# Strassen's block products for two up-projection quarters, and weight block sums made by accumulating DMAs

## The chip, the cores and the metric

One of the eight cores of a Trainium2 chip runs the whole program. The metric is device time in microseconds (us) for one execution; of the kernel before there are three timed runs and one profiled execution. The engines are named as in the profile: PE (matmuls), PEld (its weight loads), DVE (vector), ACT (scalar), POOL (GpSimd) and SP, which here only issues DMAs.

## What is computed

A decoder trunk of two layers on 512 tokens of 1024 features. Each layer has a mixer (a convolution with a state-space scan in the first, gated linear attention in the second), cross-attention into 256 memory tokens, and an MLP, each followed by a LayerNorm of `ALPHA * x + f(x)`. The change is about the MLP, of which the reference says:

```
def sq_relu_mlp(x, w1, w2):
    return jnp.square(jax.nn.relu(x @ w1)) @ w2

h = layer_norm(DEEPNORM_ALPHA * h + sq_relu_mlp(h, mlp_w1[i], mlp_w2[i]), ln_g[i, 2], ln_b[i, 2])
```

`w1` is 1024 x 4096, `w2` is 4096 x 1024, all in float32.

## The kernel before

**Three matmuls for one.** Each operand is held as a pair in a rounded form that PE takes at full rate: `hi`, a cast copy made on ACT, and `lo`, the rest, made on DVE as source minus `hi` (`split`, L104 to L107). A product is then hi x hi, hi x lo and lo x hi (`mm3`, L156 to L160). Weights come from DRAM by 1 MB loads on SP's queue and pass through `wpair`: two pieces of 128x1024 for each megabyte, one ACT cast and one DVE subtraction each. The pools for these pieces (`wh`, `wl`) hold six each.

**The up projection** makes feature tiles: the weight pair is the stationary operand, the 512 tokens stream past. A quarter of the 4096 features is 8 tiles x 8 pieces of the inner dimension x 3 = 192 matmuls of 512 columns (`feat_tiles`). ACT then does Relu and Square on each tile and writes it into a tile `ab`. The first four tiles of a quarter 0 are made in two halves of 256 tokens (`halves=4`), because the second half of the tokens is still being transposed.

**The down projection** takes the first three quarters by one level of Strassen's algorithm in Winograd's form (`strassen`, L537 to L587). A quarter's 1024x1024 weights are cut into four blocks of 512x512, its 512 tokens into two halves, and seven block products of 24 matmuls with 512 columns do what eight would. The sums of weight blocks are DVE subtractions (`blk_sub`, L524 to L527, in two pieces of 128x1024 each, four sums in a quarter). The sums of activation blocks are DVE instructions too (L567 to L577), and so are the additions of the products into the residual tiles `h` and the shared product `E` (L547 to L559). The last quarter goes through `out_proj`, whose LayerNorm follows.

**What sets the order.** The instructions of each engine are laid down in one order when the program is built, by a list scheduler that knows the data dependences; at run time each engine takes its own in that order and waits on semaphores. Between the block products of a quarter lie the up tiles of the next (`mlp`: two tiles of quarter `qd + 1` ahead of `strassen`, six behind it), so that in the built order they can mix.

Of the kernel before, what the change touches and what calls it, by code (L numbers as in the profile page):

```python
# [22 lines left out]
ALPHA = (2 * DEPTH) ** 0.25  # L23
# [6 lines left out]
class Trunk:  # L30
# [253 lines left out]
    def bcast_row(self, row, tag):  # L284
        t = self.cp.tile([P, D], F32, tag=tag, name=self.nm(tag))
        self.nc.sync.dma_start(t, row.rearrange("(o d) -> o d", o=1).broadcast_to([P, D]))
        return t
# [7 lines left out]


    def begin_ln(self, i, j):
        g = self.bcast_row(self.aps["ln_g"][i, j], "lng")
        b = self.bcast_row(self.aps["ln_b"][i, j], "lnb")
# [118 lines left out]
    def xa(self, i, h, xT, kT, v):  # L418
# [78 lines left out]

    def blk_load(self, w, r, c, stays=True):  # L500
# [14 lines left out]
    def sa(self, shape):
        return self.mp.tile(shape, F32R, tag="sa", bufs=4, name=self.nm("sa"))

    def blk_a(self, src):
        t = self.sa([P, 2, 4, 256])
# [16 lines left out]
    def strassen(self, w, r0, A, h, E, first, last):  # L536
# [4 lines left out]
        X = self.blk_load(w, r0, 0)  # L541

        def add(t, hf, begin):
            def f(i, ps):
                y = h[t + i, hf]
                if begin and first:
                    v.scalar_tensor_tensor(y, y, ALPHA, ps, ALU.mult, ALU.add)  # L547
                else:
                    v.tensor_tensor(y, y, ps, ALU.add)
# [11 lines left out]
        pa = [self.ps.tile([P, S], F32, tag="acc", name=self.nm("acc")) for _ in range(2)]  # L561
        self.blk_prod(pa, self.blk_a(A1[:, :, t0]), self.blk_w(X), True, e1)
        self.blk_prod(pa, self.blk_a(A2[:, :, t0]), self.blk_w(self.blk_load(w, r0 + S, 0, False)), False, add(0, 0, True))
        B12 = self.blk_load(w, r0, S)
        self.blk_sub(X, B12, X)
        Sx = self.mp.tile([P, 4, 256], F32, tag="sx", bufs=2, name=self.nm("sx"))
        v.tensor_tensor(Sx, A1[:, :, t1], A2[:, :, t1], ALU.add)  # L567
        pc = [self.accb() for _ in range(2)]
        self.blk_prod(pc, self.blk_a(Sx), self.blk_w(X), True, add(2, 1, True))
        B22 = self.blk_load(w, r0 + S, S)  # L570
        self.blk_sub(X, B22, X)
        v.tensor_tensor(Sx, Sx, A1[:, :, t0], ALU.subtract)
        pb = [self.aux() for _ in range(2)]
        self.blk_prod(pb, self.blk_a(Sx), self.blk_w(X), True, e2)
        self.blk_sub(B12, B22, B12)
        v.tensor_tensor(Sx, A2[:, :, t0], Sx, ALU.subtract)
        v.tensor_tensor(A1[:, :, t1], A1[:, :, t0], A1[:, :, t1], ALU.subtract)  # L577
        self.blk_prod(pc, self.blk_a(Sx), self.blk_w(B22), False, add(0, 1, True))
        self.blk_sub(X, self.blk_load(w, r0 + S, 0, False), X)
        pd = [self.ps.tile([P, S], F32, tag="acc", name=self.nm("acc")) for _ in range(2)]  # L580
        self.blk_prod(pd, self.blk_a(A1[:, :, t1]), self.blk_w(B12), True, add(2, 1, False))
        self.blk_prod(pd, self.blk_a(A2[:, :, t1]), self.blk_w(X), False, add(2, 0, True))
        if last:
            for i in range(2):
                for y in (h[i, 1], h[2 + i, 1], h[2 + i, 0]):
                    v.tensor_tensor(y, y, E[i], ALU.add)

    def mlp(self, i, h, xT):
        nc = self.nc
        w1, w2 = self.aps["mlp_w1"][i], self.aps["mlp_w2"][i]  # L590
        NQ = 4
        A = {}

        r2 = []

        def pair(m):
            if m % 4 == 0:
                hl = [self.sa([P, 4, S]) for _ in range(2)]
                r2.extend([(hl[0][:, k, :], hl[1][:, k, :]) for k in range(4)])
            self.split(A[NQ - 1, m // 4][:, m % 4, :], *r2[m])  # L600

        def up(qd, m0, n, halves=0, pairs=False):
# [693 lines left out]
```

## Time and profile before

| | us |
|---|---|
| timed runs | 1610.10, 1605.85, 1609.43 (median 1609.43) |
| the profiled execution, its own time | 1611.48 |
| its span from first to last instruction | 1609.8 |
| PE busy | 1581.7 (98%) |
| DVE busy | 1067.8 (66%) |
| ACT busy | 703.7 (44%) |
| POOL busy | 338.6 (21%) |
| DMA queues, share of 16 engines' span | 35.2% (SP's queue) |

The profile is of one execution. Busy shares are over the whole span; a matmul's duration includes the time in which it overlaps its neighbours, so the pace of PE is read from the starts of successive matmuls. The MLP of layer 0 takes about 543 to 876 us of the span, that of layer 1 has the same form near the end.

### The profile page before, as it was taken

To read this page: it belongs to the slowest core of one execution; us is meant where nothing else is said; L and a number is where in the kernel's file an instruction comes from. 1 tells how busy PE (TensorE), PEld (TensorE's weight loads), DVE (VectorE), ACT (ScalarE), POOL (GpSimd) and SP (SyncE) were. 2 spreads that over 40 slices of the span, in tenths; PEclk is the share of its full clock that TensorE was granted. 3 is DMA by queue.
4 is the path that set the end of the run, shared out by engine and by line. 5 is a ranking of instruction groups with operands and counts; after the bars stand their busy time and mean duration, and the time that the engine had idled before them with its cause. 6 is when DMAs were issued, how large, how long until landed. Compare 5 with 4: busy or idle time off the path is not lost.

```text
span 1609.8 us, 19786 instructions
## 1 busy us (share of the span) xinstructions
PE 1581.7 (98%) x7866; PEld 1327.8 (82%) x7866; DVE 1067.8 (66%) x1372; ACT 703.7 (44%) x1087; POOL 338.6 (21%) x266
## 2 busy tenths in 40 slices
PE   8999999999999999999999999999999999999998
PEld 7878888788988988888888788898988988888886
DVE  3997999883755676676837544444754767676835
ACT  3346547661332454545442534352342354545440
POOL 5745837744101200000001121222201200000000
PEclk9999999999999999999999999999999999999999
DMA  7223336633521515152233331267321525242221
GB/s 250 97 80 107 104 105 190 200 108 105 209 79 52 185 53 183 53 166 70 79 105 98 118 105 60 98 217 248 98 93 32 191 66 166 70 157 79 79 79 53
DMA packets 136864, 188.50 MB, mean 117 GB/s; under 512 B 6966, under 2 KB 82918, under 8 KB 136771
## 3 DMA queue, kind: packets, MB, share of 16 engines
q1 hardware_dynamic: 136162, 187.03, 35.2%
q8 instruction: 62, 1.02, 0.3%
q0 software_dynamic: 608, 0.20, 0.1%
q14 instruction: 32, 0.25, 0.0%
HBM read 176.69 MB, written 10.52 MB: 116 GB/s over the span
## 4 chain that ended last, share of the span: by engine, by line
PE 90%; DVE 5%; DMA 2%; POOL 1%; issue 1%; ACT 1%; SPq 0%; DVEq 0%; POOLq 0%; ACTq 0%
PE acc L159 18%; PE acc L160 18%; PE acc L158 18%; PE accb L160 8%; PE accb L159 8%; PE accb L158 8%; DVE cv L948 2%; PE aux L160 2%; PE aux L158 2%; PE aux L159 2%; DVE h L319 1%; DMA ws<-in_even_w_in_dram 1%; PE aux L279 1%; PE aux L874 1%; DMA t<-acsd 0%
## 5 line engine op out<-in xcount | busy, mean ns | idle before, releaser
L106 ACT CAST wh<-ws 128x1024 fp32r<-128x1024 f32 x238 | 249.1, 1051 | 420.5 <-PE acc L160 122.5
L107 DVE TENSOR_TENSOR wl<-ws,wh 128x1024 fp32r<-128x1024 f32 x178 | 224.8, 1266 | 255.8 <-ACT wh L106 255.8
L159 PE MATMUL acc<-t,wh 128*128 128x512 f32 (+1 forms) x800 | 288.8, 362 | 3.9 <-POOL t L374 3.1
L158 PE MATMUL acc<-t,wh 128*128 128x512 f32 (+1 forms) x800 | 290.0, 364 | 0.3 <-ACT t L106 0.3
L160 PE MATMUL acc<-t,wl 128*128 128x512 f32 (+1 forms) x800 | 289.8, 363 | 0.0
L107 POOL TENSOR_TENSOR wl<-ws,wh 128x1024 fp32r<-128x1024 f32 x60 | 148.3, 2481 | 297.1 <-ACT wh L106 286.3
L159 PEld LDWEIGHTS acc<-t,wh 128*128 128x128 f32 x800 | 154.0, 193 | 26.1 <-POOL t L374 3.3
L158 PEld LDWEIGHTS acc<-t,wh 128*128 128x128 f32 x800 | 153.3, 192 | 23.2 <-issue 1.6
L160 PEld LDWEIGHTS acc<-t,wl 128*128 128x128 f32 x800 | 153.7, 192 | 22.2 <-issue 1.0
L158 PE MATMUL acc<-wh,t 128*128 128x512 f32 x424 | 168.3, 397 | 0.5 <-ACT t L106 0.5
L159 PE MATMUL acc<-wl,t 128*128 128x512 f32 x424 | 167.3, 395 | 0.0
L160 PE MATMUL acc<-wh,t 128*128 128x512 f32 x424 | 166.5, 397 | 0.3 <-DVE t L107 0.3
L948 DVE SCALAR_TENSOR_TENSOR cv<-u,cw,cv 128x491 f32<-128x491 f32 (+29 forms) x210 | 146.6, 729 | 1.0
L160 PE MATMUL accb<-t,wl 128*128 128x512 f32 (+1 forms) x368 | 126.9, 345 | 0.0
L158 PE MATMUL accb<-t,wh 128*128 128x512 f32 (+1 forms) x368 | 126.6, 345 | 0.0
L159 PE MATMUL accb<-t,wh 128*128 128x512 f32 (+1 forms) x368 | 126.6, 344 | 0.0
L106 ACT CAST wh<-sq 128x1024 fp32r<-128x1024 f32 x72 | 75.2, 1049 | 96.5 <-PE acc L160 34.0
L314 POOL TENSOR_TENSOR s<-s,mhalf 128x1 f32<-128x1 f32 x24 | 23.2, 967 | 429.9 <-DVE s L313 429.9
L107 DVE TENSOR_TENSOR wl<-sq,wh 128x1024 fp32r<-128x1024 f32 x72 | 87.6, 1221 | 35.2 <-ACT wh L106 35.2
L106 ACT CAST t<-aux 128x512 fp32r<-128x512 f32 (+1 forms) x84 | 44.8, 547 | 147.2 <-PE aux L279 121.7
L158 PE MATMUL acc<-wh,sa 128*128 128x512 f32 x272 | 107.5, 395 | 0.0
L160 PE MATMUL acc<-wh,sa 128*128 128x512 f32 x272 | 107.4, 395 | 0.0
(336 smaller groups left out, 3006.2 us busy)
## 6 DMA issues: line engine op xcount, KB each, us to landing
ws<-in_mlp_w_dram SPq DMA_DIRECT2D x52, 1024.0 KB, 5.3
sq<-in_mlp_w_dram SPq DMA_DIRECT2D x18, 1024.0 KB, 5.1
ws<-in_even_w_in_dram SPq DMA_DIRECT2D x17, 1024.0 KB, 5.1
ws<-in_odd_w_in_dram SPq DMA_DIRECT2D x12, 1024.0 KB, 5.1
ws<-in_xa_w_k_dram SPq DMA_DIRECT2D x8, 1024.0 KB, 4.9
ws<-in_xa_w_v_dram SPq DMA_DIRECT2D x8, 1024.0 KB, 5.5
kvd<-kv SPq DMA_DIRECT2D x32, 256.0 KB, 3.2
ws<-in_even_w_out_dram SPq DMA_DIRECT2D x8, 1024.0 KB, 5.0
```

The lines of the kernel that those rows point to most:

```text
L106: self.last_hi = nc.scalar.copy(hi, src)
L107: (eng or nc.vector).tensor_tensor(lo, src, hi.bitcast(F32), ALU.subtract)
L158: nc.tensor.matmul(out, a[0], b[0], start=start, stop=False, skip_group_check=more)
L159: nc.tensor.matmul(out, a[0], b[1], start=False, stop=False, skip_group_check=more)
L160: nc.tensor.matmul(out, a[1], b[0], start=False, stop=stop, skip_group_check=more)
L279: nc.tensor.transpose(ps[:, j * P:(j + 1) * P], halves[hf][:, j * P:(j + 1) * P], self.ident)
L314: nc.gpsimd.tensor_tensor(r, r, self.mhalf[:, :1], ALU.pow)
L319: nc.vector.scalar_tensor_tensor(y, y, r, ln["b"][:, sl], ALU.mult, ALU.add)
L874: last = nc.tensor.matmul(py[:, i * 64:(i + 1) * 64], Ms[i // 4][:, (i % 4) * P:(i % 4 + 1) * P], xdt[:, i * 64:(i + 1) * 64], start=True, ...
L948: nc.vector.scalar_tensor_tensor(cs[j][:, s:], u[m][:, :S - s], w[:, 30 - s:31 - s], cs[j][:, s:], ALU.mult, ALU.add)
```

## The change

Quarters 1 and 2 of the up projection become seven block products as well (`up_blocks`). Here the transposed activations are the moving operand, so a block product has 256 tokens as columns: 2 x 2 feature tiles x 4 pieces x 3 = 48 matmuls of 256 columns. The activation sums, which are the same for both quarters, are made once in a layer (`up_sums`). One function, `blk_unit`, runs the seven products for up and down in the order 1, 2, 5, 7, 6, 3, 4. The signs are arranged so that every weight sum is an addition, and `blk_sub` is gone: the tile X holds block 11 for product 1, then takes on block 12 (product 5), block 22 (product 6) and block 21 (product 4), each by a DMA with `accum_op=ALU.add` that POOL issues (`blk_add`). The tile T3 takes one such addition ahead of product 7. A unit so has four plain loads of 1 MB and four accumulating ones; there are three down units and two up units in a layer, 40 accumulating DMAs in all.

The rows of `ln_g` and `ln_b` for the MLP's LayerNorm move to a tile of the tag `sq`. The final quarter's up tiles now all follow the last down unit; no up tiles stand between block products any more.

The core of the diff:

```diff
-    def blk_sub(self, dst, a, b):
-        for j in range(2):
-            ks = slice(2 * j, 2 * j + 2)
-            self.nc.vector.tensor_tensor(dst[:, ks, :], a[:, ks, :], b[:, ks, :], ALU.subtract)
+    def blk_add(self, st, w, r, c):
+        self.nc.gpsimd.dma_start(st, w[r:r + S, c:c + S].rearrange("(k p) c -> p k c", p=P), accum_op=ALU.add)
...
+    def blk_unit(self, w, r, c, prod, op, out):
+        X = self.blk_load(w, r, c)
+        T3 = self.blk_load(w, r, c + S)
+        self.blk_add(T3, w, r + S, c + S)
+        pa = [self.ps.tile([P, S], F32, tag="acc", name=self.nm("acc")) for _ in range(2)]
+        prod(pa, op(1), self.blk_w(X), True, out[1])
+        self.blk_add(X, w, r, c + S)
+        prod(pa, op(2), self.blk_w(self.blk_load(w, r + S, c, False)), False, out[2])
+        pc = [self.accb() for _ in range(2)]
+        prod(pc, op(5), self.blk_w(X), True, out[5])
+        self.blk_add(X, w, r + S, c + S)
+        pd = [self.ps.tile([P, S], F32, tag="acc", name=self.nm("acc")) for _ in range(2)]
+        prod(pd, op(7), self.blk_w(T3), True, out[7])
+        pb = [self.aux() for _ in range(2)]
+        prod(pb, op(6), self.blk_w(X), True, out[6])
+        self.blk_add(X, w, r + S, c)
+        prod(pc, op(3), self.blk_w(self.blk_load(w, r + S, c + S, False)), False, out[3])
+        prod(pd, op(4), self.blk_w(X), False, out[4])
+    def blk_prod_t(self, pss, a, w, start, evac):
+        for i in range(2):
+            for j in range(2):
+                m = slice((2 * i + j) * P, (2 * i + j + 1) * P)
+                o = pss[i][:, j * 256:(j + 1) * 256]
+                for k in range(4):
+                    self.mm3(o, (w[k][0][:, m], w[k][1][:, m]), (a[0][:, k, :], a[1][:, k, :]),
+                             start and j == 0 and k == 0, k == 3, not start or j == 1)
+            evac(i, pss[i])
...
+        A = self.ab()
+        up(A, 0, 0, 4, halves=4)
+        ops = self.up_sums(tiles)
+        up(A, 0, 4, 4)
         for qd in range(NQ - 1):
-            last = qd == NQ - 2
-            up(qd + 1, 0, 2)
-            self.strassen(w2, qd * D, [A[qd, 0], A[qd, 1]], h, E, qd == 0, last)
-            if last:
-                pair(0)
-                pair(1)
-            up(qd + 1, 2, NK - 2, pairs=last)
+            if qd > 0:
+                A = self.ab()
+                self.up_blocks(w1, qd * D, ops, A)
+            self.down_blocks(w2, qd * D, A, h, E, qd == 0, qd == NQ - 2)
+        A = self.ab()
+        up(A, (NQ - 1) * D, 0, NK, pairs=True)
```

**The built order, on DVE.** First the kernel before, in the second block quarter of layer 0 (`sq` holds weight blocks, `wl` is a `lo` piece, in brackets the semaphores waited for; DMAHW are those of SP's DMAs, DMASW those of POOL's):

```order
L107 TENSOR_TENSOR wl_5821<-sq_5813,wh_5820 128x1024 [waits DMAHW3_49,PE_49,Activation_49]
L527 TENSOR_TENSOR sq_5813<-sq_5893,sq_5813 128x1024 [waits DMAHW4_49,DVE_49]
L527 TENSOR_TENSOR sq_5893<-sq_5938,sq_5893 128x1024 [waits DMAHW5_49,DVE_49]
L107 TENSOR_TENSOR wl_5825<-sq_5813,wh_5824 128x1024 [waits PE_49,Activation_49]
L527 TENSOR_TENSOR sq_5813<-sq_5893,sq_5813 128x1024 [waits DVE_49]
L527 TENSOR_TENSOR sq_5893<-sq_5938,sq_5893 128x1024 [waits DVE_49]
```

Then the changed kernel (its line numbers are some 90 higher), in the second down unit of layer 0, from product 5's weights to product 6's; `sq_5952` is X, `sq_5954` is T3:

```order
L107 TENSOR_TENSOR wl_6044<-sq_5952,wh_6043 128x1024 [waits DMASW4_49,Activation_49]
L107 TENSOR_TENSOR wl_6048<-sq_5952,wh_6047 128x1024 [waits Activation_49]
L650 TENSOR_TENSOR E_4830<-E_4830,acc_5957 128x512 [waits PE_49]
L663 TENSOR_TENSOR sx_6038<-ab_5506,ab_5507 128x1024 [waits Activation_49]
L107 TENSOR_TENSOR wl_6085<-sq_5954,wh_6084 128x1024 [waits DMASW2_49,DVE_49,Activation_49]
L650 TENSOR_TENSOR E_4831<-E_4831,acc_5958 128x512 [waits PE_49]
L665 TENSOR_TENSOR ab_5506<-ab_5506 128x4x256 [waits DVE_49]
L107 TENSOR_TENSOR wl_6089<-sq_5954,wh_6088 128x1024 [waits Activation_49]
L107 TENSOR_TENSOR sa_6040<-sx_6038,sa_6040 128x1024 [waits Activation_49]
L643 TENSOR_TENSOR h_2877<-h_2877,acc_5957 128x512 [waits PE_49]
L107 TENSOR_TENSOR wl_6125<-sq_5952,wh_6124 128x1024 [waits DMASW5_49,Activation_49]
```

The subtractions of line 527 are gone. The two pieces of X for product 5, and later those for product 6, now wait for a DMA of POOL's; eight instructions stand between the second piece for product 5 and the first for product 6.

**The built order, on POOL.** The kernel before has no DMA of POOL's in the MLP. The changed one has 20 in each layer; the first five of layer 0, where `sq_5222` is the first unit's X and `sq_5224` and `sq_5512` are the T3 of the first and second units:

```order
L526 DMA sq_5224<-in_mlp_w_dram 128x4x512 [waits DMAHW3_49,DMASW3_49]
L526 DMA sq_5222<-in_mlp_w_dram 128x4x512 [waits DMAHW7_49,DMAHW2_49,DVE_49]
L526 DMA sq_5222<-in_mlp_w_dram 128x4x512 [waits DMASW4_49,DVE_49]
L526 DMA sq_5512<-in_mlp_w_dram 128x4x512 [waits DMAHW7_49,DMASW3_49,DVE_49]
L526 DMA sq_5222<-in_mlp_w_dram 128x4x512 [waits DMASW5_49,DVE_49]
```

Additions to X wait for the DVE pieces that read it; the second unit's T3 stands ahead of the first unit's last addition to X.

**The built order, on PE.** In the up quarter 1, before (`t_718` to `t_721` are the activations' pairs):

```order
L159 MATMUL acc_5694<-t_721_4446,wh_5686 128x512
L160 MATMUL acc_5694<-t_720_4445,wl_5687 128x512
L158 MATMUL accb_5721<-t_718_4443,wh_5690 128x512 [waits Activation_49]
L159 MATMUL accb_5721<-t_719_4444,wh_5690 128x512
L160 MATMUL accb_5721<-t_718_4443,wl_5691 128x512 [waits DVE_49]
```

and now, in the first product of the same quarter:

```order
L159 MATMUL acc_5515<-t_719_4444,wh_5521 128x256
L160 MATMUL acc_5515<-t_718_4443,wl_5522 128x256
L158 MATMUL acc_5516<-t_718_4443,wh_5517 128x256 [waits DVE_49]
L159 MATMUL acc_5516<-t_719_4444,wh_5517 128x256
L160 MATMUL acc_5516<-t_718_4443,wl_5518 128x256
```

Tiles of 512 tokens have become tiles of 256, with the same loads of a stationary operand for each matmul.

## Rows read from the trace of the kernel before

**Rows 1.** The page, part 1: busy time, share of the span, instructions.

```profile
PE 1581.7 (98%) x7866; PEld 1327.8 (82%) x7866; DVE 1067.8 (66%) x1372; ACT 703.7 (44%) x1087; POOL 338.6 (21%) x266
```

**Rows 2.** The page, part 4: the chain that ended last, by engine.

```profile
PE 90%; DVE 5%; DMA 2%; POOL 1%; issue 1%; ACT 1%; SPq 0%; DVEq 0%; POOLq 0%; ACTq 0%
```

**Rows 3.** Waits of PE over the whole span: us in total, times, longest.

```profile
PE aux L279 <- DMA h<-in_x_dram: 6.4, 2, 3.6
PE acc L159 <- POOL t L374: 3.1, 1, 3.1
```

**Rows 4.** Windows of layer 0's MLP: length, busy us (instructions) by engine, PEclk, DMA share, GB/s.

```profile
543.00:587.00 44.00, 44.00 (x267) 39.53 (x267) 22.33 (x24) 21.45 (x29) 0.92 (x1) 1.00 0.35 121
587.00:625.00 38.00, 38.00 (x166) 30.92 (x165) 33.38 (x34) 20.04 (x23) 0.00 (x0) 1.00 0.40 134
...
668.00:708.00 40.00, 40.00 (x175) 32.57 (x174) 36.33 (x37) 20.39 (x22) 0.00 (x0) 1.00 0.41 132
```

**Rows 5.** PE timeline, columns per matmul at the end: start us, us, engine, line.

```profile
553.17 0.28 PE L158 MATMUL acc<-t,wh 128*128 128x256 f32 x1
...
561.09 0.28 PE L160 MATMUL acc<-t,wl 128*128 128x256 f32 x1
...
566.46 0.39 PE L158 MATMUL accb<-t,wh 128*128 128x512 f32 x1
...
590.94 0.39 PE L158 MATMUL acc<-t,wh 128*128 128x512 f32 x1
```

**Rows 6.** Tile sq, the weight blocks: count, duration ns min/median/max, first and last start.

```profile
L106 ACT CAST wh<-sq x72: 1037/1049/1055, 566.4 to 1508.1; 128x1024 fp32r<-128x1024 f32 x72
L107 DVE TENSOR_TENSOR wl<-sq,wh x72: 1215/1220/1226, 567.5 to 1510.2; 128x1024 fp32r<-128x1024 f32 x72
L527 DVE TENSOR_TENSOR sq<-sq,sq x36: 1216/1226/1228, 568.8 to 1488.8; 128x1024 f32<-128x1024 f32 x36
...
L527 DVE TENSOR_TENSOR sq<-ws,sq x12: 1218/1219/1226, 600.4 to 1496.7; 128x1024 f32<-128x1024 f32 x12
...
DMA to landing us min/median/max: 4.9/5.1/11.0
```

**Rows 7.** DVE timeline in layer 0's first block product.

```profile
611.64 1.22 DVE L107 TENSOR_TENSOR wl<-sq,wh 128x1024 fp32r<-128x1024 f32 x1
612.78 0.68 DVE L547 SCALAR_TENSOR_TENSOR h<-h,accb 128x512 f32<-128x512 f32 x1
613.38 1.22 DVE L107 TENSOR_TENSOR wl<-sq,wh 128x1024 fp32r<-128x1024 f32 x1
```

**Rows 8.** ACT by line and form, 550 to 790 us: busy us, mean ns.

```profile
L609 ACT ACTIVATE ab<-ab 128x512 f32<-128x512 f32 x26 | 16.5, 634 | 0.8
...
L608 ACT ACTIVATE ab<-acc 128x512 f32<-128x512 f32 x15 | 8.9, 590 | 0.0
...
L554 ACT COPY E<-acc 128x512 f32<-128x512 f32 x2 | 1.2, 588 | 1.2 <-PE acc L160 1.2
```

**Rows 9.** DMA issues: count, KB each, median us from issue to landing.

```profile
ws<-in_mlp_w_dram SPq DMA_DIRECT2D x52, 1024.0 KB, 5.3
sq<-in_mlp_w_dram SPq DMA_DIRECT2D x18, 1024.0 KB, 5.1
...
t<-in_even_conv_w_dram POOLq DMA_DIRECT2D x2, 62.0 KB, 5.5
...
c<-in_even_d_skip_dram POOLq DMA_DIRECT2D x1, 8.0 KB, 4.8
```

**Rows 10.** POOL timeline: two of the issues of its own DMAs.

```profile
4.33 0.54 POOL L687 DMA_DIRECT2D t<-in_even_conv_w_dram  x1
...
14.14 0.53 POOL L697 DMA_DIRECT2D c<-in_even_d_skip_dram  x1
```

**Rows 11.** Window with three block loads, columns as in rows 4.

```profile
612.00:624.00 12.00, 12.00 (x53) 9.73 (x52) 10.35 (x12) 4.81 (x5) 0.00 (x0) 1.00 0.73 260
```

More of the change, by code (lines that the diff above doesn't have):

```diff
@@ L282, in transpose_in, with ln_rows @@
             self.split(psv, tiles[0][hf][:, :, sl], tiles[1][hf][:, :, sl])
[L284 to L287, printed above, removed]
+    def ln_rows(self, j):
+        if j == 2:
+            t = self.mp.tile([P, 2, D], F32, tag="sq", bufs=3, name=self.nm("sq"))
+            return t[:, 0, :], t[:, 1, :]
+        return [self.ep.tile([P, D], F32, tag=n, bufs=1, name=self.nm(n)) for n in ("lng", "lnb")]
     def rstd(self, var, n, scale=1.0, eps=EPS):
@@ L297, in begin_ln @@
     def begin_ln(self, i, j):
-        g = self.bcast_row(self.aps["ln_g"][i, j], "lng")
-        b = self.bcast_row(self.aps["ln_b"][i, j], "lnb")
+        g, b = self.ln_rows(j)
+        for r, n in ((g, "ln_g"), (b, "ln_b")):
+            row = self.aps[n][i, j]
+            self.nc.sync.dma_start(r, row.rearrange("(o d) -> o d", o=1).broadcast_to([P, D]))
         return dict(g=g, b=b, y={}, st={}, h={}, out=(i == DEPTH - 1 and j == 2))
@@ L513, in blk_w, with blk_a @@
         return r
[L515 to L519, printed above, removed]
+    def blk_a(self, src, tag="sa", bufs=2):
+        t = self.mp.tile([P, 2, 4, 256], F32R, tag=tag, bufs=bufs, name=self.nm(tag))
         hi, lo = t[:, 0, :, :], t[:, 1, :, :]
@@ L534, in blk_prod @@
             evac(i, pss[i])
-    def strassen(self, w, r0, A, h, E, first, last):
+    def blk_unit(self, w, r, c, prod, op, out):
[16 more added lines that the diff above has]
+        prod(pd, op(4), self.blk_w(X), False, out[4])
@@ new lines, in blk_prod_t, with up_sums @@
+    def blk_prod_t(self, pss, a, w, start, evac):
[7 more added lines that the diff above has]
+            evac(i, pss[i])
+    def up_sums(self, tiles):
+        nc = self.nc
+        v = nc.vector
+        t0, t1 = slice(0, 256), slice(256, 512)
+        blk = lambda k, t: (tiles[0][k][:, :, t], tiles[1][k][:, :, t])
+        A11, A12, A21, A22 = blk(0, t0), blk(1, t0), blk(0, t1), blk(1, t1)
+        tmp = self.mp.tile([P, 2, 4, 256], F32, tag="sq", bufs=3, name=self.nm("sq"))
+        a, b = tmp[:, 0, :, :], tmp[:, 1, :, :]
+        c = self.mp.tile([P, 4, 256], F32, tag="sx", bufs=1, name=self.nm("sx"))
+        whole = lambda d, s: v.tensor_tensor(d, s[0].bitcast(F32), s[1].bitcast(F32), ALU.add)
+        ops = {1: A11, 2: A12, 4: A22}
+        whole(a, A21)
+        whole(b, A22)
+        v.tensor_tensor(b, a, b, ALU.subtract)
+        ops[5] = self.blk_a(b, "S0", 1)
+        whole(c, A11)
+        v.tensor_tensor(a, c, a, ALU.subtract)
+        ops[7] = self.blk_a(a, "S1", 1)
+        v.tensor_tensor(c, b, c, ALU.subtract)
+        ops[6] = self.blk_a(c, "S2", 1)
+        whole(a, A12)
+        v.tensor_tensor(a, a, c, ALU.add)
+        ops[3] = self.blk_a(a, "S3", 1)
+        return ops
@@ new lines, in ab, with up_blocks, act, o3 @@
+    def ab(self):
+        return [self.mp.tile([P, 4, S], F32, tag="ab", bufs=2, name=self.nm("ab")) for _ in range(2)]
+    def up_blocks(self, w, c, ops, A):
+        nc = self.nc
+        v = nc.vector
+        t0, t1 = slice(0, 256), slice(256, 512)
+        E = [self.mp.tile([P, 2, 256], F32, tag="E1", bufs=2, name=self.nm("E1")) for _ in range(2)]
+        v2 = lambda ps: ps.rearrange("p (m t) -> p m t", t=256)
+        dst = lambda h, t, i: A[h][:, 2 * i:2 * i + 2, t]
+        def act(d, src=None):
+            nc.scalar.activation(d, d if src is None else src, AF.Relu)
+            nc.scalar.activation(d, d, AF.Square)
+        def o3(i, ps):
+            d = dst(1, t0, i)
+            v.tensor_tensor(d, v2(ps), E[i], ALU.subtract)
+            act(d)
+        def o4(i, ps):
+            d = dst(0, t1, i)
+            v.tensor_tensor(d, v2(ps), E[i], ALU.add)
+            act(d)
+        def o6(i, ps):
+            v.tensor_tensor(E[i], E[i], v2(ps), ALU.add)
+            d = dst(1, t1, i)
+            v.tensor_tensor(d, d, E[i], ALU.subtract)
+            act(d)
+        def o7(i, ps):
+            d = dst(1, t1, i)
+            v.tensor_tensor(d, d, v2(ps), ALU.subtract)
+        out = {1: lambda i, ps: nc.scalar.copy(E[i], v2(ps)), 2: lambda i, ps: act(dst(0, t0, i), v2(ps)),
+               5: lambda i, ps: nc.scalar.copy(dst(1, t1, i), v2(ps)), 7: o7, 6: o6, 3: o3, 4: o4}
+        self.blk_unit(w, 0, c, self.blk_prod_t, ops.get, out)
@@ L537, in strassen, with down_blocks @@
+    def down_blocks(self, w, r, A, h, E, first, last):
         nc = self.nc
@@ L540, in strassen, with add @@
         t0, t1 = slice(0, 256), slice(256, 512)
-        X = self.blk_load(w, r0, 0)
-        def add(t, hf, begin):
+        def add(t, hf, begin, op=ALU.add):
             def f(i, ps):
@@ L546, in f @@
                 if begin and first:
-                    v.scalar_tensor_tensor(y, y, ALPHA, ps, ALU.mult, ALU.add)
+                    v.scalar_tensor_tensor(y, y, ALPHA, ps, ALU.mult, op)
                 else:
-                    v.tensor_tensor(y, y, ps, ALU.add)
+                    v.tensor_tensor(y, y, ps, op)
             return f
@@ L559, in e2 @@
             v.tensor_tensor(E[i], E[i], ps, ALU.add)
[L561 to L582, printed above, removed]
+        Sx = []
@@ new lines, in op @@
+        def op(n):
+            if n == 1:
+                return self.blk_a(A1[:, :, t0])
+            if n == 2:
+                return self.blk_a(A2[:, :, t0])
+            if n == 5:
+                Sx.append(self.mp.tile([P, 4, 256], F32, tag="sx", bufs=1, name=self.nm("sx")))
+                v.tensor_tensor(Sx[0], A1[:, :, t1], A2[:, :, t1], ALU.subtract)
+            if n == 7:
+                v.tensor_tensor(A1[:, :, t1], A1[:, :, t0], A1[:, :, t1], ALU.subtract)
+                return self.blk_a(A1[:, :, t1])
+            if n == 6:
+                v.tensor_tensor(Sx[0], Sx[0], A1[:, :, t0], ALU.subtract)
+            if n == 3:
+                v.tensor_tensor(Sx[0], A2[:, :, t0], Sx[0], ALU.add)
+            if n == 4:
+                return self.blk_a(A2[:, :, t1])
+            return self.blk_a(Sx[0])
@@ L583, in strassen @@
+        self.blk_unit(w, r, 0, self.blk_prod, op,
+                      {1: e1, 2: add(0, 0, True), 5: add(2, 1, True), 7: add(2, 1, False, ALU.subtract),
+                       6: e2, 3: add(0, 1, True), 4: add(2, 0, True)})
         if last:
             for i in range(2):
-                for y in (h[i, 1], h[2 + i, 1], h[2 + i, 0]):
-                    v.tensor_tensor(y, y, E[i], ALU.add)
+                for y, op in ((h[i, 1], ALU.subtract), (h[2 + i, 1], ALU.subtract), (h[2 + i, 0], ALU.add)):
+                    v.tensor_tensor(y, y, E[i], op)
@@ L591, in mlp, with up @@
         NQ = 4
-        A = {}
+        tiles = self.xT_tiles
         r2 = []
[L596 to L602, printed above, removed]
+        def up(A, c, m0, n, halves=0, pairs=False):
             def evac(j, ps):
                 m = m0 + j
-                if m % 4 == 0:
-                    A[qd, m // 4] = self.mp.tile([P, 4, S], F32, tag="ab", bufs=3, name=self.nm("ab"))
-                r = A[qd, m // 4][:, m % 4, :]
+                r = A[m // 4][:, m % 4, :]
                 nc.scalar.activation(r, ps, AF.Relu)
```

9 lines of the change are left out of this document (6 added, 3 removed).

## The prediction

> **What bounds the kernel now.** I read the page's busy shares and its chain first: PE is busy for 98% of the span [rows 1], and 90% of the chain that ended last is PE's [rows 2]. Then the waits of PE, to see whether it is ever held up: the longest is 6.4 us in two pieces at the very start, the next 3.1 us [rows 3], and neither lies in an MLP. Then the windows of the MLP: in each stretch PE is busy for the whole of it at the full granted clock, while DVE is at 33.4 of 38.0 us in a stretch of block products and at half in a stretch of up tiles [rows 4]. So in the MLP nothing but the number and width of matmuls sets the time, and the change can gain only there. It can lose wherever another engine or a DMA becomes later than PE.
>
> **PE: what the change removes.** The pace comes from starts. From 566.46 to 590.94 us there are 108 matmuls of 512 columns, 0.2267 us each; from 553.17 to 561.09 us there are 66 of 256 columns in the same form that the new products have (weights stationary, tokens moving), 0.120 us each [rows 5]. Half the columns cost 53%, not 50%. An up quarter was 192 x 0.2267 = 43.5 us and becomes 7 x 48 = 336 matmuls x 0.120 = 40.3 us. Four quarters (two in each layer) give 4 x 3.2 = **12.8 us**. This is all that the change can bring. The Trainium skill (TensorE: Matmul & The Clock Gate, "Back-to-back issue gap") lists 262 and 518 cycles for the two widths, which would make the saving 4 x (41.5 - 36.7) = 19 us; the rows of this kernel differ, and they decide.
>
> **DVE and ACT: what moves off and on.** DVE's pace is 1.14 us for 1024 elements and 0.60 us for 512 [rows 7]. The subtractions of weight blocks go: 36 + 12 instructions [rows 6], 55 us of DVE. PE did not wait for them, so by themselves they are worth nothing. Added are the activation sums, eight additions and four `lo` pieces in a layer, 12 x 1.14 = 13.7 us; they fall into the first up quarter, where DVE has 22.3 of 44 us busy [rows 4], and cost nothing. A down unit asks DVE for 25 long instructions (14 weight pieces, 7 activation pieces, 4 sums) and 14 short ones, 28.5 + 8.4 = 36.9 us, beside 7 x 24 x 0.2267 = 38.1 us of PE. An up unit asks for 14 long and 10 short, 22.0 us beside 40.3 us. ACT has in a down unit 21 casts of 1.05 us [rows 6], and in an up unit 14 casts, eight pairs of 0.59 and 0.63 us and four copies of 0.59 us [rows 8], 27 us: covered. If DVE waited for nothing, PE would stay the bound, though in down units by 1.2 us only. The rows of the LayerNorm are loaded 43 us before their use: nothing.
>
> **The accumulating DMAs: the price that the trace does not show.** Forty DMAs of 1 MB add to a tile in place. Nearest from below is a plain load of the same block on SP's queue, 5.1 us from issue to landing [rows 9]; the nearest row from above is the slowest of these loads, 11.0 us [rows 6]. POOL's own DMAs in this trace carry 62 KB and less; POOL spends about 0.5 us on an issue [rows 10], close to nothing here, and even these small ones take 4.8 to 5.5 us to land [rows 9], at the busy start of the program. A gain below 5.1 us is excluded: the block must still come from DRAM. I take more than a load, because such a DMA needs the old content of the tile as well: two megabytes are fetched to write one. What a megabyte costs on the wire: while three block loads ran, 260 GB/s moved at a share of 0.73 of the DMA engines [rows 11], so 356 GB/s at full share and 2.95 us for 1.05 MB. With the second megabyte at the price of the first, my estimate is 5.1 + 2.95 = **8.1 us** alone, and 5.9 us of wire. The Trainium skill (Collectives: The Full Stack, "The bandwidth ceiling: the fold count and why AG ≠ RS ≠ AR") says that a reducing transfer runs at half the rate of a copy because of its two source reads. No row here shows that rule; it would give the same 5.9 us.
>
> **Who waits for them.** In a unit X goes through three additions in a row. Each can start only when DVE has read the last piece of X, and only when it has landed can ACT cast the next piece (1.05 us, [rows 6]) and DVE go on. So each opens a hole on DVE of 8.1 + 1.05 = 9.15 us, filled only by what the built order has put there. Counted there, the three holes of a down unit hold 3 long and 4 short, 5 long and 3 short, 4 long and 4 short instructions: 5.8, 7.5 and 7.0 us. DVE stands idle for 3.35 + 1.65 + 2.15 = 7.2 us, and the unit takes it 36.9 + 7.2 = 44.1 us. An up unit's holes hold 2 long and 3 short, 2 long, and 3 long and 2 short: 4.1, 2.3 and 4.6 us; idle 16.4, together 38.4 us, still inside PE's 40.3. Behind a waiting piece stands all of DVE: the other pieces, and the additions that free PSUM for PE.
>
> **Collisions.** All transfers run on the same DMA engines. That they stretch each other is seen in the loads of one kind that take 5.1 us by the median and 11.0 at worst [rows 6]. In a unit the three additions to X have 3 x 5.9 = 17.7 us of wire, and the others (four loads of 2.95, one addition to T3) also 17.7 us. If they fall independently over a unit of some 48 us, 17.7 x 17.7 / 48 = 6.5 us of the one lie over the other, and sharing delays X by as much. A down unit becomes 44.1 + 6.5 = 50.6 us, 12.5 over PE's 38.1; an up unit 44.9 us, 4.6 over.
>
> **The sum.** A layer has 3 x 12.5 + 2 x 4.6 = 46.7 us of lateness. It starts with a lead: the pools hold weight pieces of three products, so DVE can be two ahead, 10.9 us. What is left, 35.8 us, PE waits, in both layers 71.6 us. Against the 12.8 us that is +58.8 us. The profiled execution took 1611.48 us, which gives 1670.3; it lay 2.05 us above the median of the timed runs, so I forecast **1668 us**.
>
> **Rivals.**
> *The additions land like loads.* Then a hole is some 6.2 to 7.2 us and mostly full. The point that decides: with no collisions PE starts to wait when three down units eat the lead of 10.9 us, at 4.8 us idle in each, a hole of 8.4 us, a landing of 7.3 us. Below that the whole 12.8 us come in: 1609.43 - 12.8 = 1596.6 us. For it speaks that the loads have 5.1 us, that the DMA engines are at 0.35 to 0.41 in these stretches [rows 4], and that DVE loses 55 us of work. Against it, that the tile must be read. This is the other side of my forecast.
> *Two reads, but no collisions.* A down unit is 6.0 us over, an up unit not at all: (18.0 - 10.9) x 2 - 12.8 = +1 us, 1611 us, no change. It needs the loads to fall between the additions; but the SP queue issues a load as soon as a tile is free, which is just when X starts on an addition. The Trainium skill (DMA: Bandwidth & Descriptors, "Issuing engines are not separate DMA queues") says that DMAs of any issuer interleave on the same 16 engines; by that rule this case is the less likely.
> *Much slower.* If an addition takes 11.0 us alone, holes of 12.05 us make down units 52.8 and up units 47.2 us: (3 x 14.7 + 2 x 6.9 - 10.9) x 2 - 12.8 = +81 us, and with 6.5 us of collisions in ten units +146 us, 1755 us.
>
> **How the numbers follow.** My forecast's case, two reads with collisions: 0.60, with a range of its own from 1625 to 1715 us (collisions of a third to about twice as much). Additions like loads: 0.25. Two reads without collisions: 0.09, of which 0.02 goes to faster, 0.05 to no change, 0.02 to slower. Much slower: 0.06. Within 0.3% (4.8 us) is about what a measurement of this kernel cannot tell from no change. Faster is 0.27, no change 0.05, slower 0.68. The range has to take in the second case, so it runs from 1593 to 1715 us; outside lie most of the last case and the ends of the first two, some 0.16.
>
> **What would show it.** The landing of `sq<-in_mlp_w` issued by POOL: 8 us and more for my forecast, under 7 us for the first rival. Waits of PE in the MLP, now none: on DVE's and ACT's pieces of `wl` and `wh`, some 36 us in each layer, and DVE or ACT in turn waiting for `sq` from a DMA. DMA share in the MLP of 0.6 to 0.75, against some 0.4. The pace of 256 columns in the new products must be 0.120 us; at more, even the first rival falls. I am wrong if PE stays without waits there, whatever the landing; and wrong in the mechanism if it waits for evacuations of PSUM without DVE waiting for X.

## The result and the profile after

| | median us (lowest to highest) | ratio to before, 95% interval |
|---|---|---|
| before | 1608.45 (1605.85 to 1610.1) | |
| changed | 1695.38 (1691.83 to 1697.34) | 1.053 (1.0517 to 1.0544) |

The change makes the kernel 87 us slower, where 58.8 us and a time of 1668 us were forecast. The profiled execution took 1695.9 us (span 1694.2). Its page, parts 1 and 4, against [rows 1] and [rows 2]:

```profile
PE 1600.4 (94%) x8442; PEld 1362.4 (80%) x8442; DVE 1090.1 (64%) x1412; ACT 735.7 (43%) x1135; POOL 390.1 (23%) x306
...
PE 41%; DMA 13%; DVE 5%; ACT 3%; issue 2%; POOL 1%; SPq 0%; DVEq 0%; ACTq 0%; POOLq 0%
```

The two chains can't be compared share by share: this one is followed back only to 622.46 us, where POOL issues a DMA, so its shares add up to some 65% of the span and not to 100%. In it transfers have 13%, where they had 2%; the page gives 12% to `sq<-in_mlp_w_dram`, which there stands for POOL's additions and SP's loads of the same tiles together. The DMA issues and the queue of POOL (answering to [rows 9]) tell the two apart:

```profile
sq<-in_mlp_w_dram POOLq DMA_DIRECT2D x40, 1024.0 KB, 8.8
sq<-in_mlp_w_dram SPq DMA_DIRECT2D x20, 1024.0 KB, 6.0
...
q0 software_dynamic: 21728, 42.15, 14.5%
```

An accumulating DMA lands after 8.8 us by the median (forecast 8.1). POOL's queue held 14.5% of 16 engines' 1694.2 us for the forty, 6.1 us each (forecast 5.9). Waits of layer 0's MLP, 540 to 900 us, read from POOL backwards, close a circle:

```profile
POOL sq L526 <- DVE wl L107: 172.8, 13, 23.9
DVE wl L107 <- ACT wh L106: 129.1, 40, 11.4
ACT wh L106 <- DMA sq<-in_mlp_w_dram: 103.8, 14, 12.7
```

The addition waits for DVE's last piece of X, DVE for ACT's cast, ACT for the addition. PE over the whole span, against [rows 3], where none of these lines stood:

```profile
PE acc L158 <- DVE E L650: 18.0, 4, 5.2
PE accb L158 <- ACT sa L106: 15.7, 4, 5.8
PE acc L158 <- DVE ab L615: 10.5, 4, 3.3
...
PE acc L158 <- ACT sa L106: 5.0, 2, 2.7
PE acc L158 <- ACT wh L106: 5.0, 4, 2.3
```

These are 54 us; with four smaller lines of the MLP (3.9, 3.7, 1.9, 1.1) 65 us. That is less than the loss, 87 us and the 12.8 us that should have been saved. The windows of the MLP, columns as in [rows 4]:

```profile
543.00:587.00 44.00, 44.00 (x261) 39.12 (x260) 30.91 (x30) 25.54 (x35) 3.94 (x3) 1.00 0.67 181
587.00:625.00 38.00, 35.29 (x148) 28.35 (x147) 27.70 (x30) 16.21 (x17) 3.82 (x3) 0.96 0.71 165
625.00:668.00 43.00, 37.32 (x292) 36.40 (x292) 14.88 (x16) 15.01 (x19) 3.88 (x3) 0.96 0.75 170
668.00:718.00 50.00, 37.19 (x163) 30.23 (x161) 35.34 (x39) 25.33 (x31) 5.16 (x4) 0.88 0.72 168
...
770.00:822.00 52.00, 42.58 (x177) 33.78 (x177) 40.35 (x45) 28.30 (x34) 3.88 (x3) 0.87 0.53 122
```

Against [rows 4] the DMA share has grown from about 0.4 to between 0.53 and 0.75, and PEclk is under 1 in every one of these stretches but the first. Finer windows around one hole, same columns:

```profile
684.00:688.00 4.00, 0.12 (x1) 0.15 (x1) 3.32 (x4) 3.97 (x7) 0.46 (x1) 0.68 0.26 99
688.00:692.00 4.00, 4.00 (x10) 3.17 (x11) 4.00 (x5) 1.95 (x3) 0.84 (x1) 0.50 0.60 94
692.00:696.00 4.00, 4.00 (x18) 3.21 (x17) 2.60 (x3) 0.00 (x0) 0.00 (x0) 0.97 1.10 234
```

From 684 to 688 us PE does almost nothing, and in the next 4 us it is granted 1.2 GHz in place of 2.4: it counts as busy throughout and begins 10 matmuls where the window after has 18. Behind a hole PE thus loses time that no wait shows. PE's timeline agrees, 0.43 us from start to start at 688, 0.23 us at 693:

```profile
688.44 0.63 PE L159 MATMUL acc<-wl,sa 128*128 128x512 f32 x1
688.87 0.63 PE L160 MATMUL acc<-wh,sa 128*128 128x512 f32 x1
...
693.21 0.39 PE L160 MATMUL acc<-wh,sa 128*128 128x512 f32 x1
693.44 0.40 PE L158 MATMUL acc<-wh,sa 128*128 128x512 f32 x1
```

Not all of this time is the kernel's loss. Where the circle around X sets the pace, slow matmuls only fill time in which PE would wait. On the chain of work that ended last, the same two paces look like this (start, us, what):

```profile
791.43 0.43 PE acc L158
...
797.38 0.24 PE acc L159
```

Only some 70 slow matmuls lie on that chain, as far back as it goes, and together they are about 14 us too long.

### The profile page after: what moved, and what is told of

Same layout as the page of the kernel before. It is cut to its first block, busy times and chain, and to the rows that moved or that the text cites. A ratio compares the mean times of both kernels' runs of the same rounds, so it can differ in the third digit from the quotient of the medians.

```text
span 1694.2 us, 21157 instructions
## 1 busy us (share of the span) xinstructions
PE 1600.4 (94%) x8442; PEld 1362.4 (80%) x8442; DVE 1090.1 (64%) x1412; ACT 735.7 (43%) x1135; POOL 390.1 (23%) x306
## 3 DMA queue, kind: packets, MB, share of 16 engines
q0 software_dynamic: 21728, 42.15, 14.5%
## 4 chain that ended last, share of the span: by engine, by line
PE 41%; DMA 13%; DVE 5%; ACT 3%; issue 2%; POOL 1%; SPq 0%; DVEq 0%; ACTq 0%; POOLq 0%
DMA sq<-in_mlp_w_dram 12%; PE acc L158 7%; PE acc L159 7%; PE acc L160 7%; PE accb L158 5%; PE accb L160 5%; PE accb L159 5%; DVE wl L107 2%; ACT wh L106 2%; DVE h L322 1%; PE aux L160 1%; PE aux L158 1%; PE aux L159 0%; POOL sq L526 0%; PE aux L1299 0%
## 5 line engine op out<-in xcount | busy, mean ns | idle before, releaser
L158 PE MATMUL acc<-t,wh 128*128 128x256 f32 (+1 forms) x856 | 293.2, 345 | 6.8 <-ACT wh L106 5.0
L160 PE MATMUL acc<-t,wl 128*128 128x256 f32 (+1 forms) x856 | 292.5, 342 | 3.7 <-DVE wl L107 3.7
L159 PE MATMUL acc<-t,wh 128*128 128x256 f32 (+1 forms) x856 | 291.1, 341 | 3.4 <-POOL t L377 3.1
L107 DVE TENSOR_TENSOR wl<-sq,wh 128x1024 fp32r<-128x1024 f32 x100 | 120.5, 1222 | 177.2 <-ACT wh L106 177.2
L106 ACT CAST wh<-sq 128x1024 fp32r<-128x1024 f32 x100 | 101.6, 1043 | 218.4 <-DMA sq<-in_mlp_w_dram 200.6
L158 PEld LDWEIGHTS acc<-t,wh 128*128 128x128 f32 x856 | 167.3, 196 | 25.6 <-ACT wh L106 6.2
L159 PEld LDWEIGHTS acc<-t,wh 128*128 128x128 f32 x856 | 168.0, 196 | 19.8 <-POOL t L377 3.4
L526 POOL DMA_DIRECT2D sq<-in_mlp_w_dram x40 | 51.7, 1308 | 471.7 <-DVE wl L107 363.6
L158 PE MATMUL acc<-wh,sa 128*128 128x512 f32 x192 | 84.2, 439 | 33.6 <-DVE E L650 18.0
L158 PEld LDWEIGHTS acc<-wh,t 128*128 128x128 f32 x400 | 75.3, 188 | 17.4 <-ACT t L106 1.4
L160 PEld LDWEIGHTS acc<-wh,t 128*128 128x128 f32 x400 | 75.2, 188 | 16.8 <-issue 1.0
L159 PEld LDWEIGHTS acc<-wl,t 128*128 128x128 f32 x400 | 75.2, 188 | 16.5 <-issue 1.0
L159 PE MATMUL acc<-wl,sa 128*128 128x512 f32 x192 | 81.9, 427 | 0.0
```

The source lines that it names most:

```text
L106: self.last_hi = nc.scalar.copy(hi, src)
L107: (eng or nc.vector).tensor_tensor(lo, src, hi.bitcast(F32), ALU.subtract)
L158: nc.tensor.matmul(out, a[0], b[0], start=start, stop=False, skip_group_check=more)
L159: nc.tensor.matmul(out, a[0], b[1], start=False, stop=False, skip_group_check=more)
L160: nc.tensor.matmul(out, a[1], b[0], start=False, stop=stop, skip_group_check=more)
L526: self.nc.gpsimd.dma_start(st, w[r:r + S, c:c + S].rearrange("(k p) c -> p k c", p=P), accum_op=ALU.add)
```

## The experiments

All runs are timed beside the kernel before. The theory is that the loss comes from the chain of `wl`, addition, `wh` on one tile X, lengthened by the landing. Rivals: the bytes on the DMA engines, POOL's queue, DVE in order, or the new products on PE.

**No sums, and plain copies.** The first run leaves the body of `blk_add` out (`pass`), the second drops the accumulation, so neither makes the block sums:

```diff
-        self.nc.gpsimd.dma_start(st, ...rearrange(...), accum_op=ALU.add)
+        self.nc.gpsimd.dma_start(st, ...rearrange(...))
```

> Leaves out all sums of weight blocks: the 40 accumulating DMAs are gone, everything else stands. My theory (PE's matmuls are the bound as soon as X need not wait): 1608.5 - 12.8 = 1596 us, between 1592 and 1600, PE without waits in the MLP and at the full granted clock there. Rival (the 256-column products, their evacuations or the missing up tiles between the products cost time by themselves): 1605 us or more, with waits of PE for DVE's or ACT's evacuations.

> The 40 DMAs of POOL stay where they are, with the same waits, but copy instead of adding (the block sums are left out, X becomes the last block loaded). My theory (the second read of the tile makes them slow and makes them collide): packets of 2 KB take some 84 ns instead of 178, landing 5.5 to 6.5 us, pairs on the wire 6 us instead of 13.5, time 1596 to 1605 us. Rival (POOL's queue and its 1.3 us of issue are the cause, not the adding): landing stays above 8 us and the time above 1670 us.

Measured: 1598.83 us, 0.9938 (0.9923 to 0.9952), and **1596.75 us, 0.9926 (0.9911 to 0.9941)**; their intervals overlap. The second run's engines, POOL's queue, DMA issues, and the largest wait of PE that is left in the MLP:

```profile
PE 1565.3 (98%) x8442; PEld 1341.2 (84%) x8442; DVE 1089.8 (68%) x1412; ACT 738.7 (46%) x1135; POOL 369.2 (23%) x306
...
q0 software_dynamic: 11488, 42.15, 7.8%
...
sq<-in_mlp_w_dram POOLq DMA_DIRECT2D x40, 1024.0 KB, 5.6
```

```profile
PE acc L158 <- ACT sa L106: 0.9, 2, 0.4
```

In the first run, without any DMAs for the sums, PE has no waits in the MLP. In the second the same forty DMAs with the same waits and bytes, without the addition, land in 5.6 us, hold the queue 7.8% of 1594.7 us, 3.1 us each, and PE waits 0.9 us in the two MLPs. So 98.6 us (1695.38 - 1596.75) are the accumulation's, and POOL's queue as such falls. The Trainium skill (Collectives: The Full Stack, "The bandwidth ceiling: the fold count and why AG ≠ RS ≠ AR") gives two source reads as the reason why a reduce-scatter between cores has half the rate of an all-gather, which copies; 6.1 against 3.1 us of wire is the same factor. No run here shows the second read itself: the profile counts 42.15 MB for either queue, and the addition also moves in 21728 packets what the copy moves in 11488, so that the copy's packets are twice as large, and not quicker as I had expected (some 0.17 against 0.18 us each). The products themselves bring 11.9 us of the 12.8 forecast by this run, and 9.8 us by the first.

**The T3 sum by DVE.** Ten of the forty go: a plain load into `ws` and two DVE additions in their place.

```diff
+    def eng_add(self, st, w, r, c):
+        t = self.blk_load(w, r, c, False)
+        for j in range(2):
+            ks = slice(2 * j, 2 * j + 2)
+            self.nc.vector.tensor_tensor(st[:, ks, :], st[:, ks, :], t[:, ks, :], ALU.add)
...
-        self.blk_add(T3, w, r + S, c + S)
+        self.eng_add(T3, w, r + S, c + S)
```

> Only T3's sum goes back to DVE (a plain load and two additions of 128x1024), so 30 accumulating DMAs stay, all in X's chain. My theory: no two additions share the wire any more, each lands after 8 to 9 us, a unit takes some 45.5 us instead of 51, in a layer 5 x 45.5 - 195 - 10.9 = 22 us of waits: 22 x 2 - 12.8 = +30, 1638 us, between 1620 and 1650. Rival (an addition alone is what counts, the pair does not): within 10 us of 1695.

Measured: 1662.39 us, 1.0321 (1.0299 to 1.0344). That is a gain of 33 us, but 24 us less than expected and outside the range. The collision itself is real: in the changed kernel's chain the third addition to X, issued within 2 us of the T3 addition of the next unit, took (start, us, what)

```profile
650.70 14.19 DMA sq<-in_mlp_w_dram
```

That was gone in this run, but its DMA issues, and its chain from 615 to 720 us, still show the additions:

```profile
sq<-in_mlp_w_dram POOLq DMA_DIRECT2D x30, 1024.0 KB, 8.9
```

```profile
619.13 9.12 DMA sq<-in_mlp_w_dram
...
632.14 10.60 DMA sq<-in_mlp_w_dram
642.81 6.85 issue
649.67 9.83 DMA sq<-in_mlp_w_dram
```

Three landings a unit, 9 to 11 us here, hold the units without any collision between additions. The run is not a clean measure of the collision, though. X had landed at 642.81, but DVE's additions to T3 stand ahead of X's pieces in DVE's order, and they waited for a load:

```profile
644.42 2.36 DVE L532 TENSOR_TENSOR sq<-sq,ws 128x1024 f32<-128x1024 f32 x2 [10.26 <-DMA sq<-in_mlp_w_dram]
```

So a third of the loss went when the collision was taken away and this wait and two additions a unit were put in; what the collision costs by itself no run shows.

**All sums by POOL.** As the diff above, for all four sums, with `gpsimd` in place of `vector`.

> All 40 sums are made by POOL (two pieces of 128x1024, 2.48 us each) from blocks that SP loads ahead into the tile of the tag ws. Same products, same order, 8 plain loads in a unit. My theory (the hole between two readings of X decides, and 5 us on POOL are under the 7.3 us that the lead can bear): PE does not wait, 1596 to 1602 us, faster than both kernels. Rival (the order without up tiles between the products, or eight megabytes in a unit, is what costs): slower than 1608 us, with PE waiting for wl or wh whose loads come late.

Measured: 1656.27 us, 1.0295 (1.028 to 1.031), 60 us over the plain copies; the expectation (1596 to 1602 us) was wrong. DVE by line, 540 to 920 us, and DVE and POOL at one addition:

```profile
L107 DVE TENSOR_TENSOR wl<-ws,wh 128x1024 fp32r<-128x1024 f32 x44 | 70.0, 1602 | 45.5 <-ACT wh L106 45.5
L107 DVE TENSOR_TENSOR sa<-ab,sa 128x1024 fp32r<-128x1024 f32 x12 | 24.2, 2013 | 2.3 <-ACT sa L106 2.3
...
L646 DVE TENSOR_TENSOR h<-h,acc 128x512 f32<-128x512 f32 x14 | 9.4, 674 | 0.0
```

```profile
617.26 0.67 DVE L656 TENSOR_TENSOR E<-E,aux 128x512 f32<-128x512 f32 x1
617.86 3.04 DVE L107 TENSOR_TENSOR sa<-ab,sa 128x1024 fp32r<-128x1024 f32 x1
...
617.41 2.39 POOL L529 TENSOR_TENSOR sq<-sq,ws 128x1024 f32<-128x1024 f32 x1 [4.03 <-DVE wl L107]
```

POOL ends at 619.80; DVE's operation, begun at 617.86, ends at 620.90, 1.10 us later, about its length when alone (1.22). In between DVE made no progress. Operations with an operand in PSUM (`h`, `E`) kept their 0.67 us. The Trainium skill (SBUF — State Buffer, "🔬 SBUF: two separate sides") says that an operation of DVE with two SBUF inputs and one of GpSimd that reads SBUF exclude each other for a whole instruction. The trace agrees, and I had left it out. How much of the 60 us it makes is not shown: X also stays on POOL for 2.39 us and more a piece, and no run separates the two.

**Sums on DVE; halves.** Four runs: all sums on DVE as in the diff above; every accumulating DMA split in two, one behind each piece of X; halves with T3 on DVE; halves with T3 on POOL.

```diff
-        self.nc.gpsimd.dma_start(st, w[r:r + S, c:c + S].rearrange(...), accum_op=ALU.add)
+        for j in range(2):
+            ks = slice(2 * j, 2 * j + 2)
+            self.nc.gpsimd.dma_start(st[:, ks, :], w[r + 256 * j:r + 256 * j + 256, c:c + S].rearrange(...), accum_op=ALU.add)
```

> All 40 accumulating DMAs replaced: SP loads the block plainly into a tile of ws and DVE adds it in two operations of 128x1024 (1.22 us each by the changed kernel's rows of that shape). POOL does nothing in the sums, so neither the add's landing nor the shared slow-down of DVE beside POOL's tensor operations (in the run with POOL's sums DVE's wl rose from 1.22 to 1.55-1.60 us and its sx to 2.4) can act. Theory (the accumulating DMA's latency is the loss, DVE has room in the units): DVE's busy share in the MLP rises from 68% in the run with plain copies to about 82%, the down units get a little longer than PE's 38.1 us, and the time is about 1620 us (1603 to 1640). Rival (DVE in order is the bound once no up tiles lie between the products, whatever sums them): as the run with POOL's sums, 1650 us or more. If it is under 1603, DVE was never short and the change would have been faster without its DMAs.

> Each accumulating DMA of 1 MB in two of 512 KB, one for each piece that DVE's wl frees; same bytes, same packets, 80 issues in place of 40. Theory (the loss is the chain wl, add's landing, wh on one tile, not the bytes): the first half starts a piece of wl earlier (about 1.85 us) and lands in some 6 us in place of 8.8, while the second half runs beside the first piece's wh and wl; of the 9.9 us that a unit loses against the run with plain copies about half comes back: 1640 us (1615 to 1660). Rival (the DMA engines are full while two adds lie over each other, the adds' packets are the bound): no gain or a loss from POOL's doubled issue work (80 times about 1.3 us), 1685 us or more.

> The X sums by accumulating DMAs in halves, as in the run of halves, and the T3 sum by a plain load and two DVE additions, so that no add is issued back to back with another unit's. Theory: the two gains join, for the halves shorten the landing and the T3 move takes away the overlap of two adds once a unit: about 1612 us (1597 to 1630). Rival (bytes, not latency): as the run with the T3 sum on DVE alone, 1662.

> As the run before it, but the T3 sum by two tensor operations of POOL, 2.4 to 4.6 us each in the run with POOL's sums. They stand on POOL's queue ahead of the unit's X adds and wait there for a load, and DVE's own operations beside them get slower (1.22 to 1.6-2.4 us). Theory: some of the gain of the halves goes again to this: 1625 us (1605 to 1650), and slower than the run with T3 on DVE. Rival (DVE is short, so that taking two operations of 1.22 us a unit off it wins): faster than that run by over 5 us.

| run | us | ratio, 95% interval |
|---|---|---|
| all sums on DVE | 1625.64 | 1.0103 (1.0086 to 1.012) |
| halves | 1627.78 | 1.0119 (1.0103 to 1.0134) |
| halves, T3 on DVE | 1617.24 | 1.0053 (1.0034 to 1.0071) |
| halves, T3 on POOL | 1636.2 | 1.0166 (1.0142 to 1.019) |

Every one lies within its range. The run with halves says most. POOL's queue and the DMA issues of that run, 540 to 900 us, and the queue of the changed kernel in 540 to 910 us:

```profile
q0 software_dynamic: 10880, 20.97, 35.1%
...
sq<-in_mlp_w_dram POOLq DMA_DIRECT2D x40, 512.0 KB, 6.5
```

```profile
q0 software_dynamic: 10560, 20.97, 33.2%
```

Over the 20 sums of this layer the queue took 35.1% of 360 us, 126 us, against 33.2% of 370 us, 123 us. The same bytes, the same time on the wire, twice the issues, and 67.6 us less for the kernel: at least these 67.6 of the 98.6 us were latency in a chain and not bytes. No run divides the other 31 us. The two remedies don't add up: T3 on DVE is worth 33 us without halves and 10.5 us with them. And for T3's sum POOL's tensor operations are dearer than the DMAs that they replace (8.4 us over the halves alone).

**Each unit's sums where it has room.** Up units: all four sums on DVE. Down units: the T3 sum by one accumulating DMA (no other unit's addition lies beside it then), the X sums by halves, by DVE, or mixed.

```diff
-        self.blk_add(T3, w, r + S, c + S)
+        how[0](T3, w, r + S, c + S)
...
-        self.blk_add(X, w, r, c + S)
+        how[1](X, w, r, c + S)
...
-        self.blk_unit(w, 0, c, self.blk_prod_t, ops.get, out)
+        self.blk_unit(w, 0, c, self.blk_prod_t, ops.get, out, [self.eng_add] * 4)
...
+                       6: e2, 3: add(0, 1, True), 4: add(2, 0, True)}, [self.dma_add] + [self.blk_add] * 3)
```

Here `dma_add` is the addition of 1 MB, `blk_add` its two halves; the second run has `[self.eng_add] * 3` at the end, the third `[self.dma_add, self.eng_add, self.blk_add, self.eng_add]`.

> Each kind of unit gets the sums that its own limit leaves room for. Up units: all four sums by plain loads and DVE (20 us of DVE work and eight additions of 1.22 us beside 40.3 us of PE, no add in flight). Down units: the X sums by accumulating DMAs in halves, the T3 sum by one accumulating DMA of 1 MB, which now has no other unit's add beside it. Theory: what the run of halves with T3 on DVE still loses against the run with plain copies (20.5 us) lay in holes of both kinds of unit; those of the 4 up units go, DVE gets room in the 6 down units: 1605 us (1597 to 1615). Rival (the T3 add slows the halves wherever it is): 1618 us or more.

> As the run before it, but in the down units the three X sums are DVE's and only the T3 sum an accumulating DMA, off everybody's path. Theory (with the sums on DVE the six down units are DVE's: one sum less a unit than the run with all sums on DVE, 2 times 1.22 us times 6 = 14.6 us): 1625.6 - 14.6 = 1611 us (1602 to 1620). Rival (the run with all sums on DVE lost its time elsewhere, to the loads of ws or to PE's waits for sa): no gain on it, 1622 us or more.

> Between the two: in the down units the T3 sum by an accumulating DMA, the second X sum by two halves, the first and the third by DVE. Theory (both limits are soft: DVE gets 2.4 us of room a unit over the run before it, and one hole of an add's landing is left where that has three): 1605 us (1597 to 1614), not slower than either of the two runs it is sent with. Rival (each hole costs more than DVE's two operations): between them or above the run with the X sums on DVE.

| X sums of the down units | us | ratio, 95% interval |
|---|---|---|
| halves | **1604.15** | 0.9973 (0.9963 to 0.9983) |
| DVE | 1618.4 | 1.0063 (1.0051 to 1.0076) |
| second by halves, others by DVE | 1612.31 | 1.0017 (1.0007 to 1.0027) |

The first is the only kernel with all its sums that beats the one before, by 4 us or 0.3%. Its waits of PE in the MLP and its DMA issues:

```profile
PE accb L158 <- ACT sa L106: 4.2, 4, 1.8
...
sq<-in_mlp_w_dram POOLq DMA_DIRECT2D x36, 512.0 KB, 6.4
sq<-in_mlp_w_dram POOLq DMA_DIRECT2D x6, 1024.0 KB, 9.3
```

The T3 addition lands as late as ever (9.3 us) and costs next to nothing, for in layer 0 ACT waits only 2.3 us for DMAs into `sq` tiles, against 103.8 us in the changed kernel: the place in the chain makes the price. The third run came out between its neighbours, not ahead of them as I had expected: in a down unit two DVE operations cost more than the hole of two halves. Per sum and unit the steps are 8.2 us / 12 = 0.7 and 6.1 us / 6 = 1.0 us. The second gained half of its expected 14.6 us over all sums on DVE. Between the first two runs only the X sums of the down units differ, 14.3 us in favour of the halves; that the up units do better with DVE's sums was not tried by itself.

## Why the prediction was right, and which terms were off

The direction and the mechanism came true: the additions land after more than 8 us, DVE and ACT wait for X, and PE waits for them. That the time lies in the range says less, for the range was 122 us wide and took in a gain. PE lost 98.6 us where my sum had 71.6, and most of the difference lies in the up units.

- **PE's saving**, 12.8 us: 11.9 us measured with plain copies, 9.8 us without the DMAs. The pace held. Of the new products in that run 138 matmuls start from the first to the last of these rows, 0.119 us apart:

```profile
625.62 0.28 PE L158 MATMUL acc<-t,wh 128*128 128x256 f32 x1
...
641.92 0.28 PE L159 MATMUL aux<-S,wh 128*128 128x256 f32 x1
```

- **Subtractions that leave DVE, worth nothing**: so it was; without the additions' latency nothing came but PE's share.
- **Landing 8.1 us, wire 5.9 us**: 8.8 and 6.1 us. Both estimates stood on a second read; the plain copies show that the accumulation makes the difference, though not that it does so by this read. The rival of additions that land like loads falls (its point was 7.3 us), though its time was right for plain copies: 1596.6 forecast, 1596.75 measured. An issue on POOL takes 1.31 us, not the 0.5 us of [rows 10].
- **Collisions, random, 6.5 us in every unit**: wrong in kind. The T3 addition and the third to X are issued within 3.6 us of each other in every unit but the last of a layer, so the overlap is built in. The second rival, without collisions, falls with it. "Much slower" needed 11.0 us for an addition alone; with T3's sum on DVE the median is 8.9 us.
- **The up unit, 44.9 us**: the term that was furthest off. From the first addition to X of one unit to that of the next, on POOL's timeline, up units took 52.0 us twice and a down unit 50.3 us (forecast 50.6):

```profile
622.46 1.27 POOL L526 DMA_DIRECT2D sq<-in_mlp_w_dram  x1 [22.87 <-DVE h L641]
...
674.48 1.28 POOL L526 DMA_DIRECT2D sq<-in_mlp_w_dram  x1 [22.50 <-DVE wl L107]
...
724.78 1.28 POOL L526 DMA_DIRECT2D sq<-in_mlp_w_dram  x1 [20.73 <-DVE wl L107]
...
776.75 1.28 POOL L526 DMA_DIRECT2D sq<-in_mlp_w_dram  x1 [23.88 <-DVE wl L107]
```

DVE's timeline of the up unit at 622 us shows why:

```profile
632.64 1.23 DVE L107 TENSOR_TENSOR wl<-sq,wh 128x1024 fp32r<-128x1024 f32 x1 [6.97 <-ACT wh L106]
...
647.93 2.36 DVE L107 TENSOR_TENSOR wl<-sq,wh 128x1024 fp32r<-128x1024 f32 x2 [10.06 <-ACT wh L106]
...
666.07 2.36 DVE L107 TENSOR_TENSOR wl<-sq,wh 128x1024 fp32r<-128x1024 f32 x2 [9.92 <-ACT wh L106]
```

Three idles make 27 us, where I had 16.4 and 6.5 of collision. From the start of each issue to DVE's next piece of X the holes last 10.2, 12.0 and 15.4 us, together 37.5 us instead of 3 x 9.15 + 6.5 = 33.9; the third addition is the one of 14.2 us in the chain above. The other half of the 7.1 us lies between the holes, 14.5 us where I had counted 22.0 - 11.0 = 11.0 of work: 8.4 us pass from product 4's pieces to the next unit's first addition. In layer 1, at 1394.30, 1444.89, 1494.83 and 1545.30 us on the same timeline, up units took 50.6 and 50.5 us and the down unit 49.9. With these lengths my own sum gives 3 x 12.2 + 2 x 11.7 - 10.9 = 49.1 us of stall in layer 0 and 45.0 us in layer 1, 94 of the 98.6 us measured; the first and the last unit of a layer are taken to be like the others.

- **36 us of waits a layer**: 32 us. The sum of 71.6 us looks right by this, and is not, for PE lost 98.6 us: 65 us are waits, and the rest is slower matmuls, which the prediction had put at nothing. PE is busy for 1600.4 us here and for 1565.3 us with plain copies, 35 us less for the same 8442 matmuls. The span's mean clock was 0.974, with plain copies 0.996; 1694.2 x 0.026 - 1594.7 x 0.004 = 38 us of clock, some of it in the holes themselves. By the chain above about 14 us of this lie on the path; the rest ran while the circle around X set the pace. That the additions cost 98.6 us is shown by the runs; how waits and clock share it is worked out from the profile, and no run has held the clock up.

## What to carry to other kernels

An accumulating DMA is not a free addition: 1 MB took 8.8 us to land where a copy took 5.6, and twice the wire. Put it where nothing waits for it, or cut it along the pieces that its consumer takes; where it closes a loop with its own consumer, its landing is on the path however idle the engines are. Before a sum is moved between engines, count each kind of unit by itself: here the down units, where DVE was nearly full, did better with accumulating halves than with DVE's additions by 14.3 us. And a hole in PE's work is read twice, in its waits and in the granted clock behind them; whether the second part costs anything, the chain says.

## What the runs showed of the hardware

- Half the size takes not half the landing: 512 KB in 6.5 us, 1 MB in 8.8 us. Even so, two halves, each started as soon as its piece was free, saved 67.6 us.
- The accumulation makes 21728 packets in POOL's queue of what a copy of the same bytes moves in 11488, and POOL's issue of it takes 1.31 us against 0.76 us.
- An operation of DVE with both inputs in SBUF took 3.04 us beside a POOL operation of 2.39 us, and 1.22 us alone; operations with an operand in PSUM kept their 0.67 us.
